# Strassen weight forms of a decoder step: summed, rounded and split in one instruction over all K tiles instead of two

## The chip, the cores and the metric

One core of a Trainium2 chip runs the whole step. The metric is the device time of one execution in microseconds (us); lower is better.

## The reference

Two layers of a decoder trunk on 512 prompt positions and 8 sample tokens, 520 columns in all, model width 2048. Cut to what matters here:

```python
h = rmsnorm(x, norm_g)
z = h @ w_in                                  # 2048 x 8192
b_c, c_c, x_c, g_c, q, k, v, g_r = split_projection(z)
conv_y, new_buf = short_conv(c_c * x_c, conv_buf, conv_w)
y_conv = b_c * conv_y * silu(g_c)
o, new_S = retention(rope(q), rope(k) * HD ** -0.5, v, ret_S, log_gamma)
y_ret = group_norm(o) * silu(g_r)
x = x + concat([y_conv, y_ret]) @ w_out       # 2048 x 2048
x = x + sigmoid(x @ w_pg) * (p_i @ w_ple)     # 2048 x 2048
```

All is float32, and after the layers comes a last RMSNorm. The outputs are the activations and the new convolution and retention states.

## The kernel before

**Products.** Activations are kept transposed: tiles of 128 of the 2048 features (K tiles, 16 of them) by 520 columns, handled as two halves of 260 columns. A float32 product is made of three TensorE matmuls on rounded operands: each operand is split into a high part (the value rounded to fp32r) and a low part (the rest), and `mm3` (L247 to L249) adds high x high, weights' high x activations' low, and weights' low x activations' high. The weights are the stationary side, 128 x 128, and each matmul streams 260 columns.

**Weights.** Weights come from HBM in rows of K tiles into `raw_ring`, a ring of 32 tiles of 128 x 128. `split_w` turns a stretch of it into the two parts: ScalarE writes the rounded high part (L229), VectorE subtracts it from the raw values and writes the low part (L230). Both parts lie in `split_ring`, a ring of 60 tiles, in contiguous stretches; a place is free again when TensorE has read it.

**Pairs.** Two blocks of 128 output features at a time are a pair. `plain` multiplies them directly, loading and splitting four K tiles at a time. `strassen` treats the first `s` K tiles as a 2 x 2 block product with the two output blocks and the two column halves, and needs seven products of `q = s / 2` K tiles instead of eight; the K tiles from `s` to 16 are done as in `plain`. Which pair uses which `s` is written out in tables at the top (`HEADS`, `CONVS`, `OUT_ROWS`, `GATES`): mostly 14 (q = 7) in the heads' pairs and 16 (q = 8) in the others, 8 or 12 in a few, and 0 (plain) where a stage begins or ends.

The seven weight operands of a pair (here called forms) are `w11`, `w12`, `w22` as loaded and four more that `add` (L319, on VectorE) makes in place in the raw ring as sums or differences. `times` then splits a form and multiplies it: q tiles x 3 matmuls, so 24 matmuls for eight tiles. Three constants set how many K tiles one instruction takes: `CHL` for a DMA load, `CHA` for `add`, `CHS` for `split_w` in `times`. All three are 4, so forms of five to eight tiles are handled in two pieces (3 + 4 for seven, 4 + 4 for eight):

```python
def chunks(a, b, most=CH):
    n = (b - a + most - 1) // most
    e = [a + (b - a) * i // n for i in range(n + 1)] if n else [a]
    return list(zip(e, e[1:]))

def times(out, raw, xs, start, more):
    for i, j in chunks(0, q, CHS):
        w = split_w(raw[:, P * i : P * j])
        product(out, w, 0, xs[i:j], start and i == 0, j == q, more)
        split_ring.put(*w)
```

**Stages and order.** Each layer runs the heads' pairs (with the retention steps placed beside them), the pairs of the convolution branch, the output projection, and the gate. The operands of the next stage (their loads, the sums of activation tiles L413 to L416 and their splits L551 and L552) are made while the last pairs of the stage ahead still run. The order of instructions on every engine is set at build time by a list scheduler that works from priorities and its own estimate of durations; splits and sums of weights are raised by `WPRIO`. On the chip each engine then works strictly in that order. The last part of the program (from L1281 on) is ordered by hand on TensorE and VectorE.

Of the kernel before, what the change touches and what calls it, by code (L numbers as in the profile page):

```python
# [28 lines left out]
EPS = 1e-6  # L29
NSLOT = 75  # L30
CH = 4
CHS = 4
CHA = 4
CHL = 4
CK = 256
BUSY = 10**9
# [155 lines left out]
def trunk_kernel(  # L192
# [32 lines left out]
    def split_w(raw, slot=False):  # L225
        n = raw.shape[1]
        hi, lo = (getr()[:, :n] if slot and not split_ring.fits(n // P) else split_ring.get(n // P) for _ in range(2))
        with tc.high_priority(offset=WPRIO):
            S.activation(hi, raw, AF.Copy)  # L229
            V.tensor_tensor(lo, raw, F(hi), SUB)  # L230
        return hi, lo
# [6 lines that stand above are left out]
# [52 lines left out]
    def strassen(x, src0, src1, s, step=None):  # L290
# [24 lines left out]
        def add(out, x, y, op):  # L315
            for i, j in chunks(0, q, CHA):
                n = slice(P * i, P * j)
                with tc.high_priority(offset=WPRIO):
                    V.tensor_tensor(out[:, n], x[:, n], y[:, n], op)  # L319
# [6 lines that stand above are left out]
# [1153 lines left out]
```

## Time and profile before

| what | value |
|---|---|
| three timed runs | 2166.78, 2166.96, 2170.64 us (median 2166.96) |
| profiled execution | span 2167.3 us, from the first to the last instruction; no other time of it is given |
| ScalarE rounds the high parts, L229 | 1347 instructions, 777.3 us |
| VectorE makes the low parts, L230 | 1346 instructions, 849.2 us |
| VectorE sums forms, L319 | 660 instructions, 428.9 us |

"Busy" is the time in which an engine had an instruction in work. Matmuls overlap each other, so a matmul's own duration (some 283 ns) is more than the distance of two of them. In the rows of groups, the number after the bar is the idle time of the engine just before these instructions, with what ended it. Line numbers are those of the kernel; PE is TensorE, PEld its weight load, DVE VectorE, ACT ScalarE, SP the queue that issues the weight loads.

### The profile page before, as it was taken

What the parts mean: (1) busy time and instruction counts of PE and PEld (TensorE: products, weight loads), DVE (VectorE), ACT (ScalarE), POOL (GpSimd) and SP (SyncE); (2) the same over time, 40 slices, a digit from 0 to 9 for tenths busy, and PEclk for the clock granted to TensorE, in tenths of its full rate; (3) what the DMA queues carried; (4) which work ended last, traced back from release to release, by engine and by line L of the source; (5) the groups of instructions that cost most, each with busy time, mean ns of one, the idle gap of its engine ahead of it and who ended that gap; (6) DMA issues with size and microseconds to landing.
All of it is one profiled execution on the core that took longest, in us unless ns stands there. A gap on an engine that the chain in (4) does not pass through costs nothing. (4 is left out here: it accounts for less than half of the span.)

```text
span 2167.3 us, 48178 instructions
## 1 busy us (share of the span) xinstructions
PE 2147.8 (99%) x17861; PEld 2142.1 (99%) x17861; DVE 1896.1 (87%) x3849; ACT 1264.5 (58%) x2647; POOL 430.6 (20%) x746
## 2 busy tenths in 40 slices
PE   9999999999999999999999999999999999999998
PEld 9999999999999999999999999999999999999998
DVE  8889988998999987987997988989999998879884
ACT  8656655565555655655765655565645555456565
POOL 2313222211001211200212222231111022011011
PEclk9999999999999999999999999999999999999999
DMA  8555565545543745645645566664464355566455
GB/s 288 171 175 197 181 217 184 178 157 175 158 129 118 238 156 187 215 154 160 215 144 175 172 213 191 189 209 170 151 182 149 120 158 202 176 207 200 128 164 198
DMA packets 182861, 387.31 MB, mean 179 GB/s; under 512 B 25888, under 2 KB 56352, under 8 KB 182624
## 3 DMA queue, kind: packets, MB, share of 16 engines
q1 hardware_dynamic: 128704, 212.98, 31.6%
q0 software_dynamic: 53056, 169.84, 23.8%
q8 instruction: 140, 2.29, 0.4%
q10 hardware_dynamic: 864, 1.39, 0.2%
q14 instruction: 97, 0.79, 0.1%
HBM read 318.96 MB, written 65.15 MB: 177 GB/s over the span
## 5 line engine op out<-in xcount | busy, mean ns | idle before, releaser
L247 PE MATMUL ps_g<-slot,split 128*128 128x260 f32 x5465 | 1531.6, 284 | 7.2 <-ACT slot L307 2.9
L248 PE MATMUL ps_g<-slot,split 128*128 128x260 f32 x5465 | 1534.3, 282 | 0.3 <-DVE slot L555 0.3
L249 PE MATMUL ps_g<-slot,split 128*128 128x260 f32 x5461 | 1519.9, 283 | 0.5 <-DVE split L230 0.5
L229 ACT ACTIVATE split<-raw 128x512 fp32r<-128x512 f32 (+2 forms) x1347 | 777.3, 596 | 583.1 <-DVE raw L319 213.2
L247 PEld LDWEIGHTS ps_g<-slot,split 128*128 128x128 f32 x5465 | 1024.0, 188 | 10.1 <-ACT slot L307 3.7
L248 PEld LDWEIGHTS ps_g<-slot,split 128*128 128x128 f32 x5465 | 1028.5, 188 | 0.5 <-DVE slot L555 0.5
L249 PEld LDWEIGHTS ps_g<-slot,split 128*128 128x128 f32 x5461 | 1019.8, 188 | 1.0 <-DVE split L230 1.0
L230 DVE TENSOR_TENSOR split<-raw,split 128x512 fp32r<-128x512 f32 (+2 forms) x1346 | 849.2, 652 | 172.5 <-PE ps_g L248 85.4
L319 DVE TENSOR_TENSOR raw<-raw 128x512 f32<-128x512 f32 (+1 forms) x660 | 428.9, 660 | 32.5 <-DMA raw<-wi 23.7
L307 ACT ACTIVATE slot<-ps_g 128x260 f32<-128x260 f32 x336 | 127.4, 381 | 140.6 <-PE ps_g L249 122.7
L551 ACT ACTIVATE slot<-slot 128x520 fp32r<-128x520 f32 (+1 forms) x212 | 109.2, 562 | 46.6 <-DVE slot L414 11.1
L552 DVE TENSOR_TENSOR slot<-slot,slot 128x520 fp32r<-128x520 f32 (+1 forms) x212 | 124.4, 620 | 4.1 <-ACT slot L551 3.9
L781 POOL DMA_DIRECT2D o_rets<-slot x64 | 35.3, 552 | 351.6 <-DVE slot L780 131.7
L307 DVE TENSOR_TENSOR slot<-ps_g,slot 128x260 f32<-128x260 f32 x168 | 70.9, 424 | 6.0 <-PE ps_g L249 3.7
L869 POOL DMA_DIRECT2D slot<-hs x64 | 46.2, 724 | 118.7 <-DVE split L230 42.7
L814 POOL DMA_DIRECT2D hs<-slot x64 | 35.6, 556 | 139.3 <-DVE slot L755 61.3
L780 DVE SCALAR_TENSOR_TENSOR slot<-slot,vs,slot 128x256 f32<-128x256 f32 x128 | 56.1, 481 | 4.5 <-ACT slot L776 4.3
L746 DVE TENSOR_TENSOR slot<-slot,slot 128x520 f32<-128x520 f32 x80 | 55.8, 698 | 4.7 <-DMA o_rets<-slot 3.7
L770 POOL DMA_DIRECT2D slot<-sret x64 | 35.5, 554 | 114.6 <-ACT split L229 37.3
L1058 POOL DMA_DIRECT2D slot<-x1s x76 | 40.8, 538 | 87.6 <-PE ps_g L249 27.2
L1209 POOL DMA_DIRECT2D x2s<-slot x30 | 16.4, 545 | 201.6 <-DVE slot L1204 200.6
L771 POOL DMA_DIRECT2D slot<-kq x64 | 34.9, 547 | 106.0 <-DVE slot L876 22.2
(217 smaller groups left out, 1733.8 us busy)
## 6 DMA issues: line engine op xcount, KB each, us to landing
raw<-wi SPq DMA_DIRECT2D x377, 256.0 KB, 3.9
raw<-wo SPq DMA_DIRECT2D x128, 256.0 KB, 5.4
raw<-wg SPq DMA_DIRECT2D x122, 256.0 KB, 4.1
raw<-wi SPq DMA_DIRECT2D x136, 192.0 KB, 4.0
slot<-x1s POOLq DMA_DIRECT2D x76, 260.0 KB, 5.1
slot<-sret POOLq DMA_DIRECT2D x64, 256.0 KB, 4.0
hs<-slot POOLq DMA_DIRECT2D x64, 256.0 KB, 4.0
slot<-hs POOLq DMA_DIRECT2D x64, 256.0 KB, 5.2
```

The source lines that it names most:

```text
L229: S.activation(hi, raw, AF.Copy)
L230: V.tensor_tensor(lo, raw, F(hi), SUB)
L247: PE.matmul(out, wh, xh, start=start, stop=False, skip_group_check=more)
L248: PE.matmul(out, wh, xl, start=False, stop=False, skip_group_check=more)
L249: PE.matmul(out, wl, xh, start=False, stop=stop, skip_group_check=more)
L307: fn(*args)
L319: V.tensor_tensor(out[:, n], x[:, n], y[:, n], op)
L551: keep(S.activation(hi, src[:, n], AF.Copy))
L552: V.tensor_tensor(lo, src[:, n], F(hi), SUB)
L746: V.tensor_tensor(out[:, n], v, table[:, n], MUL)
L780: keep(V.scalar_tensor_tensor(st[:, c], k, vs[:, h, e, b : b + 1], st[:, c], MUL, ADD))
L869: SIDE.dma_start(t[:, :512].rearrange("p (m n) -> p m n", m=2), src)
```

## The change

Two constants become 8, so that `add` and the split in `times` take a whole form of up to eight K tiles at once. `CHL` stays 4: a form is still loaded by two DMAs. Nothing else in the code changes; `plain`, the K tiles from `s` on, and pairs with four tiles a form work in pieces as before.

```diff
-CHS = 4
-CHA = 4
+CHS = 8
+CHA = 8
 CHL = 4
```

Since the scheduler orders the program anew, the order shifts in many places. Two of them follow, both on VectorE.

The first is in the convolution stage of the second layer, in a pair of eight tiles a form (around 1610 to 1618 us in the profile of before). `L319` sums forms, `L230` makes low parts, `L746` and `L1092` to `L1095` are work on the convolution's values. Before:

```order
2562 L319 TENSOR_TENSOR raw<-raw 128x512
2563 L230 TENSOR_TENSOR split<-raw,split 128x512 x2
2564 L746 TENSOR_TENSOR slot_1127_21089<-slot_1124_20859,slot_1127_21089 128x520
2565 L230 TENSOR_TENSOR split<-raw,split 128x512 x2
2566 L319 TENSOR_TENSOR raw<-raw 128x512
2567 L230 TENSOR_TENSOR split<-raw,split 128x512
2568 L1092 SCALAR_TENSOR_TENSOR slot_1128_21094<-slot_1127_21089,vec,slot_1128_21094 128x511
2569 L1094 SCALAR_TENSOR_TENSOR slot_1128_21094<-scv,vec,slot_1128_21094 128x8
2570 L319 TENSOR_TENSOR raw<-raw 128x512
2571 L230 TENSOR_TENSOR split<-raw,split 128x512
2572 L1093 SCALAR_TENSOR_TENSOR slot_1128_21094<-slot_1127_21089,vec,slot_1128_21094 128x510
```

The same place after the change:

```order
2000 L230 TENSOR_TENSOR split<-raw,split 128x1024
2001 L746 TENSOR_TENSOR slot_1127_19991<-slot_1124_19779,slot_1127_19991 128x520
2002 L319 TENSOR_TENSOR raw<-raw 128x1024
2003 L230 TENSOR_TENSOR split<-raw,split 128x1024 x2
2004 L1092 SCALAR_TENSOR_TENSOR slot_1128_19996<-slot_1127_19991,vec,slot_1128_19996 128x511
2005 L1094 SCALAR_TENSOR_TENSOR slot_1128_19996<-scv,vec,slot_1128_19996 128x8
2006 L230 TENSOR_TENSOR split<-raw,split 128x1024
2007 L1093 SCALAR_TENSOR_TENSOR slot_1128_19996<-slot_1127_19991,vec,slot_1128_19996 128x510
```

Where a sum of four tiles stood between the splits of halves, and other work between the halves of one form, now a whole form is summed and then split in one piece.

The second place is at the end of the convolution stage of the first layer (around 711 to 716 us in the profile of before), where the operands of the output projection are made: `L413` to `L416` are sums of activation tiles, `L552` their low parts. Before:

```order
1166 L230 TENSOR_TENSOR split<-raw,split 128x512
1167 L415 TENSOR_TENSOR slot_480_9348<-slot_478_9345,slot_477_9343 128x260
1168 L230 TENSOR_TENSOR split<-raw,split 128x384
1169 L552 TENSOR_TENSOR slot_469_9325<-slot_465_9253,slot_469_9325 128x260
1170 L230 TENSOR_TENSOR split<-raw,split 128x512
1171 L414 TENSOR_TENSOR slot_467_9319<-slot_466_9255,slot_467_9319 128x260
1172 L552 TENSOR_TENSOR slot_470_9326<-slot_465_9253,slot_470_9326 128x260
1173 L414 TENSOR_TENSOR slot_479_9347<-slot_478_9345,slot_479_9347 128x260
1174 L552 TENSOR_TENSOR slot_472_9332<-slot_466_9255,slot_471_9331 128x520
1175 L230 TENSOR_TENSOR split<-raw,split 128x256
```

After:

```order
900 L230 TENSOR_TENSOR split<-raw,split 128x896
901 L415 TENSOR_TENSOR slot_480_8853<-slot_478_8850,slot_477_8848 128x260
902 L552 TENSOR_TENSOR slot_469_8830<-slot_465_8765,slot_469_8830 128x260
903 L319 TENSOR_TENSOR raw<-raw 128x896
904 L414 TENSOR_TENSOR slot_467_8824<-slot_466_8767,slot_467_8824 128x260
905 L552 TENSOR_TENSOR slot_470_8831<-slot_465_8765,slot_470_8831 128x260
906 L552 TENSOR_TENSOR slot_472_8837<-slot_466_8767,slot_471_8836 128x520
907 L1093 SCALAR_TENSOR_TENSOR slot_462_8702<-slot_461_8697,vec,slot_462_8702 128x510
908 L1095 SCALAR_TENSOR_TENSOR slot_462_8702<-scv,vec,slot_462_8702 128x8
909 L414 TENSOR_TENSOR slot_479_8852<-slot_478_8850,slot_479_8852 128x260
910 L416 TENSOR_TENSOR slot_468_8825<-slot_466_8767,slot_467_8824 128x260
911 L230 TENSOR_TENSOR split<-raw,split 128x896 x2
```

Before, a split of weights came after every one or two pieces of other work; now seven pieces of operand and convolution work stand between the sum at 903 and the next two splits, which are whole forms of seven tiles.

The weight loads on SP keep their number and sizes, and TensorE keeps its number of matmuls, in another order.

## The prediction

> **What bounds the kernel now.** I read the page first, then the busy time by windows, the waits, the groups with shapes kept apart, and last the timeline at the few places where TensorE stands still.
>
> ```profile
> span 2167.3 us, 48178 instructions
> PE 2147.8 (99%) x17861; PEld 2142.1 (99%) x17861; DVE 1896.1 (87%) x3849; ACT 1264.5 (58%) x2647; POOL 430.6 (20%) x746
> ...
> 0.00:40.00 40.00, 37.24 (x281) 36.32 (x282) 30.33 (x56) 31.99 (x62) 13.34 (x32) 1.00 0.93 325
> 40.00:2100.00 2060.00, 2052.39 (x17104) 2048.58 (x17103) 1826.27 (x3707) 1193.50 (x2491) 405.35 (x693) 1.00 0.56 176
> 2100.00:2168.00 68.00, 58.17 (x481) 57.22 (x479) 39.53 (x90) 39.04 (x97) 11.95 (x21) 0.97 0.52 179
> ```
>
> TensorE is the bound. In the window from 40 to 2100 us it is busy for 2052.39 of 2060 us, at 2052.39 / 17104 = 0.120 us a matmul, at the full clock. The change leaves its number of matmuls alone. So the most that faster producers can win there is the idle rest, 2060.00 - 2052.39 = **7.6 us**, or 0.35% of the span; the start and the end hold no merged pieces worth a term. What the change can lose has no such lid: the question is whether TensorE will wait for pieces that are twice as large.
>
> Who is ahead of whom is in the waits:
>
> ```profile
> ACT split L229 <- DVE raw L319: 213.2, 160, 4.3
> ...
> ACT split L229 <- PE ps_g L249: 186.2, 220, 3.9
> ...
> DVE split L230 <- PE ps_g L248: 85.4, 109, 2.2
> ACT split L229 <- DMA raw<-wi: 75.6, 59, 3.5
> ```
>
> (Engine and line, who ended the wait, us in total, times, longest.) Both producers wait for TensorE to free places in the split ring, 220 and 109 times: they run ahead until the ring is full. The ring is the cover under which late loads and late sums cost nothing, and it stays at 60 tiles.
>
> **The change part by part. First, what it removes.** Its cost rows:
>
> ```profile
> L230 DVE TENSOR_TENSOR split<-raw,split 128x512 fp32r<-128x512 f32 x1031 | 695.0, 690 | 147.8 <-PE ps_g L248 81.2 <-ACT split L229 51.8 <-issue 6.1
> L229 ACT ACTIVATE split<-raw 128x512 fp32r<-128x512 f32 x1032 | 632.3, 626 | 462.3 <-DVE raw L319 188.2 <-PE ps_g L249 166.4 <-PE ps_g L248 45.1
> L319 DVE TENSOR_TENSOR raw<-raw 128x512 f32<-128x512 f32 x520 | 354.1, 688 | 17.6 <-DMA raw<-wi 12.1 <-DMA raw<-wo 2.9
> L230 DVE TENSOR_TENSOR split<-raw,split 128x384 fp32r<-128x384 f32 x249 | 137.1, 555 | 16.2 <-ACT split L229 9.9 <-PE ps_g L248 3.4 <-ACT slot L551 1.9
> ...
> L229 ACT ACTIVATE split<-raw 128x384 fp32r<-128x384 f32 x249 | 127.2, 518 | 84.0 <-DVE raw L319 25.0 <-PE ps_g L248 24.2 <-PE ps_g L249 17.9
> ...
> L319 DVE TENSOR_TENSOR raw<-raw 128x384 f32<-128x384 f32 x140 | 77.4, 554 | 14.9 <-DMA raw<-wi 11.6 <-DMA raw<-wg 2.8
> ...
> 499.70 1.89 DVE L230 TENSOR_TENSOR split<-raw,split 128x512 fp32r<-128x512 f32 x3
> ...
> 701.15 1.57 ACT L229 ACTIVATE split<-raw 128x512 fp32r<-128x512 f32 x3 [1.40 <-DVE raw L319]
> ```
>
> There are 520 + 140 = 660 sums of forms, four a pair and two each for pairs of more than four tiles a form: the rows give 47 pairs of eight tiles (512 twice), 33 of seven (384 and 512), one of six and three of four, which stay as they are. So 81 pairs lose 4 sums and 7 splits each: 891 instructions of VectorE and 567 of ScalarE.
>
> The time for one more tile is 690 - 555 = 135 ns on VectorE and 626 - 518 = 108 ns on ScalarE. No row shows eight tiles, so estimates: 690 + 4 x 135 = 1230 ns and 626 + 4 x 108 = 1058 ns. Against two single ones that saves 150 and 194 ns. Back to back, though, three splits of VectorE take 1.89 us and three of ScalarE 1.57, so each further one takes 0.60 and 0.47, and a merger saves only 0.06 and 0.04. VectorE is thus freed of 53 to 134 us and ScalarE of 23 to 110 us, between these two ends. Nearly all of it is worth nothing, because it lies beside matmuls.
>
> The Trainium skill has a rule for each side. "Advanced Engine Details and Errata", section The Read-Write Bubble, says that memory latency shows between instructions of these two engines, and advises operands of 512 or 1024 elements; by it alone the sum below would be zero or negative. "Perfetto Trace Analysis", section Optimizing Scalar/DVE Operations, says of engines that are not saturated but cause bubbles on others: "breaking up instructions may allow work to be completed sooner"; by it the change goes the wrong way. The trace bears the first out in the 0.06 us; the second bears on the places below.
>
> **What it adds: the ring holds fewer whole pieces.** An eight-tile piece takes 16 of the 60 tiles, half a piece 8. Before, 7 halves fit; with one being read and one being written, 5 are spare, each 12 matmuls: 60 x 0.120 = 7.2 us of cover. After, 3 whole pieces fit and one is spare: 24 x 0.120 = 2.9 us. Seven-tile pieces: 8 halves before, so 6 spare x 10.5 matmuls = 7.6 us; 4 whole ones after, 2 spare x 21 = 5.0 us. These are estimates from the 0.120 us; places freed tile by tile soften them a little. The cover falls by **4.3 us** in the eight-tile pairs and **2.6 us** in the seven-tile ones. In most of the run this costs nothing: the mean wait of a split for its sum is 213.2 / 160 = 1.3 us, under either cover. It costs where the cover runs out already.
>
> **Term 1: the change of operands from the convolutions to the output projection**, once a layer.
>
> ```profile
> 700.00:710.00 10.00, 8.80 (x73) 8.60 (x73) 10.00 (x20) 8.85 (x22) 3.74 (x7) 1.00 0.52 147
> 710.00:720.00 10.00, 10.00 (x86) 10.00 (x85) 10.00 (x25) 6.16 (x20) 3.54 (x7) 1.00 0.89 293
> 720.00:730.00 10.00, 7.88 (x64) 7.47 (x63) 10.00 (x22) 9.87 (x28) 3.29 (x7) 1.00 1.01 376
> ...
> 706.46 0.39 PE L247 MATMUL ps_g<-slot,split 128*128 128x260 f32 x1 [1.20 <-ACT ps_g L307]
> ...
> 726.13 0.39 PE L247 MATMUL ps_g<-slot,split 128*128 128x260 f32 x1 [0.83 <-ACT slot L307]
> 729.26 0.39 PE L247 MATMUL ps_g<-slot,split 128*128 128x260 f32 x1 [1.29 <-ACT split L229]
> ...
> 1787.85 0.39 PE L247 MATMUL ps_g<-slot,split 128*128 128x260 f32 x1 [1.29 <-ACT slot L307]
> 1795.74 0.39 PE L247 MATMUL ps_g<-slot,split 128*128 128x260 f32 x1 [0.56 <-ACT slot L307]
> ```
>
> (Windows: PE, PEld, VectorE, ScalarE and GpSimd busy, clock, DMA share, GB/s. Timeline: in brackets the idle time and who ended it.) From 700 to 730 us VectorE is full for 30 us, and the DMA engines are full in the last ten, since the next stage's operands are loaded, summed and split here. TensorE lives on the cover and runs out of it: 1.20 + 0.83 + 1.29 us here, 1.29 + 0.56 us in the second layer, 5.2 of the 7.6 us. The last pair ahead has seven tiles, so the stage begins with 2.6 us less cover. Against that stands that pair's own relief on VectorE: 11 mergers at 0.06 to 0.15 us, 0.7 to 1.7 us, of which I count half an us, since much of it falls ahead of the full stretch. Term: 2 x (2.6 - 0.5) = **+4.2 us**; its ends are 2 x -1.7 = -3.4 (the cover was not what mattered) and 2 x 2.6 = +5.2.
>
> **Term 2: a form whose second half lands late.** The longest pieces of the chain hold these loads:
>
> ```profile
> 1458.90 8.50 DMA raw<-wi
> ...
> 1614.61 3.28 DMA raw<-wi
> 1617.97 0.64 ACT split L229
> ...
> 1695.01 3.75 DMA raw<-wi
> ...
> 1717.32 3.63 DMA raw<-wi
> ...
> 1614.14 1.16 ACT L229 ACTIVATE split<-raw 128x512 fp32r<-128x512 f32 x2 [0.45 <-PE ps_g L249]
> 1617.97 0.63 ACT L229 ACTIVATE split<-raw 128x512 fp32r<-128x512 f32 x1 [2.67 <-DMA raw<-wi]
> ...
> 1618.65 0.39 PE L247 MATMUL ps_g<-slot,split 128*128 128x260 f32 x1 [0.24 <-ACT split L229]
> ```
>
> At 1614 us ScalarE splits what has landed, waits 2.67 us for the rest of a form, and TensorE multiplies the first half meanwhile: it idles for 0.24 us only. With one instruction the form waits for its last byte. TensorE then lacks the 12 matmuls of the first half as cover, 1.44 us, and the split lasts 1058 - 626 = 0.43 us longer: 1.9 us for each such load that finds the cover spent. Of the four loads in the chain I charge two (TensorE idled after the one at 1614, and the one at 1717 lies in the same run of loads): **+3.8 us**. Ends: 0, if none is late again, and 4 x 1.9 = +7.6.
>
> The loads themselves are unchanged in number and size, but a raw region is now free for its next load only when the whole piece has been read. That is up to one half-split later, about 0.6 us, hidden as long as the cover is not spent; I price it inside term 2.
>
> **Sum:** 2167.3 + 4.2 + 3.8 = 2175.3 us against the profiled execution. Its span is 0.3 us over the median of the three timed runs, 2166.96, and the profile gives no other time of it; so the forecast for the median is **2175 us**, 0.4% slower. The ends of the terms give -3.4 to +12.8.
>
> **The rivals.**
>
> *The relief wins (faster).* ScalarE ends most of the large waits quoted above with a copy out of PSUM (L307), which stands in its queue behind splits and operand work; if fewer instructions bring these copies and VectorE's operand work forward in the two full stretches, the idle time there shrinks. This decides if a stretch contains more saving than cover lost: it needs over 2.6 us, so more than 17 mergers at the best price of 0.15 us, and the pair ahead has 11. Its most is all 7.6 us, 2159; a likely case is two thirds of it, 2162. The Trainium skill's section The Read-Write Bubble speaks for it. Chance 0.10.
>
> *Nothing to be measured.* The scheduler sets the order anew, the late loads move, and the remaining cover of 2.9 to 5.0 us is enough but for an us or two: 2167 to 2170 us. For it speaks the mean wait of 1.3 us; against it that 5.2 us are lost with a cover of over 7 us already. Chance 0.28. This kernel's runs tell about 0.2%, 4.3 us, from no change.
>
> *The steady stretch fails (much slower).* If the single spare piece of the eight-tile pairs (2.9 us) is spent in each of them, because a sum waits for its load and the split for its sum (longest waits 4.3 and 3.5 us), each of the 47 pairs stalls. At 0.4 us apiece, 47 x 0.4 = 19 us: 2186. Against it: the means are far under 2.9 us, and VectorE has more free time than before. Chance 0.14.
>
> **How the numbers follow.** The forecast's own case, stalls at the changes of operands and at late loads, from 2171.4 to 2181, has 0.48. Slower by over 0.2% is this case and the steady stretch, 0.62; within 0.2% is 0.28; faster is 0.10. The range reaches from just under no change to the steady stretch at its price, 2164 to 2187, and leaves out most of the faster case and the far end of the slowest.
>
> **What would show it.** Right: TensorE's busy time stays at about 2148 us, its idle time between 40 and 2100 us grows from 7.6 to about 15 us, the growth lies around 700 to 730 and 1780 to 1800 us and behind a few raw loads, and ends in ScalarE's splits or copies; VectorE's busy time falls by 53 to 134 us without any use. Step one is wrong if an eight-tile split lasts other than about 1.23 and 1.06 us. Term 1 is wrong if the two stretches stall no more than now; term 2 if late loads are followed by no idle TensorE; all of it if short stalls come back in every eight-tile pair.

## The result and the profile after

The changed kernel takes 2229.85 us (median of four runs, 2223.70 to 2233.24) beside 2168.47 us for the kernel before: a ratio of 1.0273, 95% interval 1.0249 to 1.0298. It is **slower by 61 us**. The sign was forecast and the size was not: 2175 us, with a range that ended at 2187. The profiled execution is the shortest of the four runs, 2223.7 us with a span of 2221.7; what the views below say is about this run, whose span is 54 us longer than that of before.

The page and the busy time by windows (us of the stretch, then PE, PEld, VectorE, ScalarE and GpSimd busy with their instructions, clock, DMA share, GB/s):

```profile
span 2221.7 us, 45853 instructions
...
PE 2173.9 (98%) x17861; PEld 2152.6 (97%) x17861; DVE 1835.9 (83%) x2958; ACT 1184.0 (53%) x2080; POOL 434.9 (20%) x746
...
0.00:40.00 40.00, 38.28 (x282) 37.77 (x283) 30.50 (x56) 32.05 (x62) 13.36 (x32) 1.00 0.92 328
40.00:2150.00 2110.00, 2074.99 (x17091) 2055.95 (x17090) 1766.03 (x2823) 1111.95 (x1926) 409.50 (x693) 1.00 0.54 171
```

What the change removes came as worked out: VectorE has 3849 - 2958 = 891 instructions fewer, ScalarE 2647 - 2080 = 567. VectorE's busy time fell by 60.2 us, ScalarE's by 80.5. But TensorE's idle time in the long middle rose from 7.6 to 2110.00 - 2074.99 = **35.0 us**, and its busy time for about the same 17,100 matmuls rose too, from 2052.39 to 2074.99 us. The latter isn't work: the first matmul behind a stop counts 0.39 us and more (rows below), where a fed one starts 0.12 us after its neighbour; and a few microseconds are the clock (last section). A stop therefore costs more than the idle time that the profile puts ahead of it.

The waits, in the columns of before:

```profile
ACT split L229 <- DVE raw L319: 288.4, 123, 6.8
...
DVE split L230 <- ACT split L229: 156.4, 177, 5.0
...
DVE split L230 <- PE ps_g L248: 97.0, 58, 3.7
ACT split L229 <- DMA raw<-wi: 95.2, 64, 4.3
ACT split L229 <- PE ps_g L248: 86.4, 69, 5.4
...
ACT split L229 <- PE ps_g L249: 35.7, 22, 4.5
...
PE ps_g L247 <- ACT split L229: 16.4, 21, 2.4
```

ScalarE's waits for a free place in the split ring fell from 186.2 + 74.4 = 260.6 to 35.7 + 86.4 = 122.1 us. Its waits for sums rose from 213.2 to 288.4 us, in fewer and longer pieces, and VectorE's for ScalarE from 69.3 to 156.4. VectorE's waits for a place fell in number, from 109 to 58, but not in total (85.4 to 97.0 us). Before, the producers mostly ran ahead until the ring was full; now they wait for each other more, and run into a full ring less often. TensorE's wait for ScalarE's splits ends up in the list, 21 times.

Where the time is lost shows in the number of matmuls that TensorE gets through in equal stretches of the clock. Two of them, of before and then of after:

```profile
1150.00:1500.00 350.00, 349.33 (x2921) 348.83 (x2920) 311.56 (x692) 207.39 (x458) 89.03 (x151) 1.00 0.59 187
...
500.00:700.00 200.00, 200.00 (x1672) 200.00 (x1671) 181.12 (x359) 106.14 (x213) 23.30 (x32) 1.00 0.48 144
```

```profile
1150.00:1500.00 350.00, 336.96 (x2748) 333.27 (x2747) 282.25 (x485) 180.32 (x328) 89.73 (x152) 0.99 0.56 177
...
500.00:700.00 200.00, 197.43 (x1613) 194.09 (x1612) 174.26 (x256) 96.67 (x146) 24.43 (x34) 1.00 0.44 137
```

At 0.120 us a matmul, the heads of the second layer (1150 to 1500) lose 173 x 0.120 = **20.8 us**, the convolutions of the first (500 to 700) 59 x 0.120 = 7.1 us. (The changed kernel falls further behind as it runs, so equal stretches don't hold quite the same work.) The same count over all of the middle is in the table of the second group of experiments.

**Two kinds of stop.** The first is in the heads of the second layer. Timeline of the changed kernel at two of its largest stops:

```profile
1196.67 1.09 DVE L230 TENSOR_TENSOR split<-raw,split 128x896 fp32r<-128x896 f32 x1
...
1197.78 0.81 SPq L312 DMA_DIRECT2D raw<-wi  x2
...
1204.18 0.95 ACT L229 ACTIVATE split<-raw 128x896 fp32r<-128x896 f32 x1 [1.64 <-DMA raw<-wi]
...
1205.18 0.58 PE L247 MATMUL ps_g<-slot,split 128*128 128x260 f32 x1 [2.08 <-ACT split L229]
...
1418.41 1.09 DVE L230 TENSOR_TENSOR split<-raw,split 128x896 fp32r<-128x896 f32 x1
...
1419.52 0.82 SPq L312 DMA_DIRECT2D raw<-wi  x2
...
1424.87 2.63 ACT L229 ACTIVATE split<-raw 128x896 fp32r<-128x896 f32 x3 [3.17 <-DMA raw<-wi]
...
1425.87 0.39 PE L247 MATMUL ps_g<-slot,split 128*128 128x260 f32 x1 [2.44 <-ACT split L229]
```

And the DMA issues of the two moments (count, KB, us from issue to landing):

```profile
raw<-wi SPq DMA_DIRECT2D x1, 256.0 KB, 5.9
...
raw<-wi SPq DMA_DIRECT2D x1, 256.0 KB, 4.9
```

Both times the two loads of a form are issued 0.02 us after the low part of a whole form has ended (1196.67 + 1.09 = 1197.76, 1418.41 + 1.09 = 1419.50). The second of them goes out some 0.4 us later and lands after 5.9 and 4.9 us, at 1204.1 and 1424.8. There ScalarE goes on, and TensorE, which has long run dry, 1.0 us later. A region of the raw ring comes free only when the whole piece has been read; the load starts late, and nothing covers it. At the first of the two stops the cover was already spent: ScalarE's two splits ahead of the late one began at 1200.74, after 2.32 us of waiting for TensorE to free a place in the split ring.

The second kind is in every pair of the convolutions between 500 and 700 us. Timeline of one (`L1093` and `L1095` are work on the convolution's values):

```profile
596.61 1.22 DVE L230 TENSOR_TENSOR split<-raw,split 128x1024 fp32r<-128x1024 f32 x1
597.74 0.75 DVE L1093 SCALAR_TENSOR_TENSOR slot<-slot,vec,slot 128x510 f32<-128x510 f32 x1
598.40 0.22 DVE L1095 SCALAR_TENSOR_TENSOR slot<-scv,vec,slot 128x8 f32<-128x8 f32 x1
598.54 1.22 DVE L319 TENSOR_TENSOR raw<-raw 128x1024 f32<-128x1024 f32 x1
...
599.79 1.06 ACT L229 ACTIVATE split<-raw 128x1024 fp32r<-128x1024 f32 x1 [1.80 <-DVE raw L319]
...
597.88 0.39 PE L249 MATMUL ps_g<-slot,split 128*128 128x260 f32 x1
...
600.91 0.39 PE L247 MATMUL ps_g<-slot,split 128*128 128x260 f32 x1
```

The sums are made in place: `w21` is overwritten by w21 + w22, then by w22 - w11, then by w12 - w21. So a sum can't begin before the low part of the form in the same region has been made. This is tight once a pair: the third form follows the second at once, while two other products stand between the third and `w12 - w21`. Here the low part ends at 597.83, and TensorE starts on it 0.05 us later; the next sum begins at 598.54 and ends at 599.76, its rounding ends at 600.85, and TensorE starts on that 0.06 us later. Low part, sum, rounding: 1.22 + 1.22 + 1.06 = 3.50 us of instructions for one form, one behind the other on two engines, against 24 x 0.120 = 2.88 us of matmuls. With halves the same work can overlap, one half with ScalarE while the other is with VectorE. This was a reading of the trace; the experiments tried it.

### The profile page after: what moved, and what is told of

Read it like the earlier page. It is cut to its first block, busy times and chain, and to the rows that moved or that the text cites. A ratio compares the mean times of both kernels' runs of the same rounds, so it can differ in the third digit from the quotient of the medians.

```text
span 2221.7 us, 45853 instructions
## 1 busy us (share of the span) xinstructions
PE 2173.9 (98%) x17861; PEld 2152.6 (97%) x17861; DVE 1835.9 (83%) x2958; ACT 1184.0 (53%) x2080; POOL 434.9 (20%) x746
## 5 line engine op out<-in xcount | busy, mean ns | idle before, releaser
L230 DVE TENSOR_TENSOR split<-raw,split 128x1024 fp32r<-128x1024 f32 (+4 forms) x780 | 777.9, 1013 | 272.0 <-ACT split L229 156.4
L229 ACT ACTIVATE split<-raw 128x1024 fp32r<-128x1024 f32 (+4 forms) x780 | 679.3, 886 | 572.1 <-DVE raw L319 288.4
L319 DVE TENSOR_TENSOR raw<-raw 128x1024 f32<-128x1024 f32 (+2 forms) x336 | 385.4, 1147 | 27.7 <-DMA raw<-wi 15.1
L552 DVE TENSOR_TENSOR slot<-slot,slot 128x520 fp32r<-128x520 f32 (+1 forms) x212 | 124.4, 622 | 9.2 <-ACT slot L551 9.0
L746 DVE TENSOR_TENSOR slot<-slot,slot 128x520 f32<-128x520 f32 x80 | 55.8, 698 | 1.8 <-DMA o_retp<-slot 1.1
L307 ACT ACTIVATE ps_g<-ps_g 128x260 f32<-128x260 f32 x121 | 45.1, 373 | 21.8 <-PE ps_g L249 20.0
```

Of the source, the lines that this page charges most:

```text
L307: fn(*args)
L552: V.tensor_tensor(lo, src[:, n], F(hi), SUB)
L746: V.tensor_tensor(out[:, n], v, table[:, n], MUL)
```

## The experiments

All kernels compute the same values; times are medians of four runs (other counts are named), and ratios are against the kernel before, run beside them at 2167 to 2169 us.

### One part of the change at a time, and more room

**split_only**: only the splits are whole.

```diff
-CHA = 8
+CHA = 4
```

> Splits take a whole form, sums stay in two pieces. Raw-ring theory (a raw region is free for its next load only when the whole form has been read, and load, sum and split then follow each other in whole forms: the round trip through four regions becomes the bound): most of the loss stays, 2200 to 2220 us. Split-ring theory (fewer whole pieces fit into 60 tiles): all of it stays, 2220 to 2235. Order theory (the new order happens to be a bad one): any time, with stalls at other places.

**sum_only**: only the sums are whole.

```diff
-CHS = 8
+CHS = 4
```

> Sums take a whole form, splits stay in two pieces. Raw-ring theory: only one link of the round trip is longer, and regions are read in halves as before: 2168 to 2185 us. Split-ring theory: as before, 2165 to 2172. Order theory: any time.

**ring64**: the change with a larger split ring.

```diff
-SPLIT = 60
+SPLIT = 64
```

> The change with a split ring of 64 tiles instead of 60, so that four whole eight-tile pieces fit instead of three. Split-ring theory: most of the loss is gone, 2170 to 2190 us, and TensorE's idle time between 40 and 2150 us falls from 35 to under 15. Raw-ring theory: no more than 10 us better than the change, 2213 to 2232.

**raw40**: the change with one more region of eight tiles in the raw ring, for which the split ring has to give up four.

```diff
-RAW = 32
+RAW = 40
-SPLIT = 60
+SPLIT = 56
```

> The change with a raw ring of 40 tiles (five regions of eight instead of four); the split ring gives up four tiles for it (56), which leaves three whole eight-tile and four whole seven-tile pieces in it as in the change. Raw-ring theory: most of the loss is gone, 2170 to 2190 us, ScalarE's waits for sums fall from 288 to under 150 us and its waits for TensorE to free the split ring grow again. Split-ring theory: 2220 to 2240.

| | median us | ratio (95%) |
|---|---|---|
| split_only | 2250.15 | 1.0375 (1.0357 to 1.0392) |
| sum_only | 2191.15 | 1.0106 (1.0091 to 1.0121) |
| ring64 | 2208.25 | 1.0188 (1.0169 to 1.0206) |
| raw40 | 2231.59 | 1.0293 (1.0277 to 1.0308) |

The parts don't add up: whole splits alone cost 82 us, more than the change; whole sums alone cost 23. Both lie above every range that was named for them. Four more tiles in the split ring give back 22 of the 61 us, so the ring's room counts, but isn't all of it: 2208 us lies between the ranges of the two theories. raw40 as a whole speaks against a short raw ring as the one cause. Its waits say why the total hides something:

```profile
ACT split L229 <- DVE raw L319: 281.8, 103, 8.0
...
ACT split L229 <- DMA raw<-wi: 35.5, 17, 4.2
```

The late loads of the first kind are nearly gone (95.2 to 35.5 us), and the waits for sums are not.

### The chain of sums

To test the second kind, the third sum gets a region of its own, so that it waits for no low part, and `w21` is given back early.

```diff
+        u = raw_ring.get(q)
+        add(u, w22, w11, SUB)
...
+        raw_ring.put(w21)
...
-        add(w21, w22, w11, SUB)
-        times(a, w21, t2, False, True)
+        times(a, u, t2, False, True)
...
-        add(w21, w12, w21, SUB)
+        add(u, w12, u, SUB)
...
-        times(b, w21, at(ops, k2, RIGHT), False, True)
-        raw_ring.put(w21)
+        times(b, u, at(ops, k2, RIGHT), False, True)
+        raw_ring.put(u)
```

**apart32** is the changed kernel with this edit.

> The change, with the third sum of a pair (w22 - w11) written to a free region of the raw ring instead of over the second one (w21); its region then takes w12's load. Chain theory (sums are made in place, so the sum for the third form waits until the second form has been split by both engines, and with whole forms ScalarE and VectorE take turns instead of overlapping): at least 12 us better than the change, 2190 to 2215 us, and ScalarE's waits for sums fall from 288 us to under 230. Ring theory (only the number of whole pieces in the split ring counts): 2222 to 2235.

**apart40** also has the rings of raw40 (40 raw, 56 split).

> The same with a raw ring of 40 and a split ring of 56 tiles, so that w12 need not wait for a region. Chain theory: better than the run with 40 raw tiles alone (2231.6) by at least 12 us, 2190 to 2217 us. Ring theory: 2225 to 2240.

**before_apart32** is the kernel before with the edit.

> The kernel before, with the third sum in a region of its own. Halves overlap on the two engines already, so by the chain theory little is won: 2162 to 2170 us. By the ring theory nothing: 2165 to 2171.

**before_raw40** is the kernel before with 40 raw and 56 split tiles.

> Control: the kernel before with 40 raw and 56 split tiles, in halves. Seven halves of eight tiles and seven-tile pairs' halves fit as before. Chain theory and ring theory both: 2163 to 2173 us; if it is over 2180, the 56 tiles cost something by themselves and the runs with 40 raw tiles have to be read against it.

**before_apart40** has both (seven runs).

> The kernel before with 40 raw and 56 split tiles and the third sum in a region of its own, in halves. Chain theory: the halves overlapped already, so 2160 to 2170 us, at best a few us under before (its TensorE idles 7.6 us between 40 and 2100 us, which is the most that can be won). Ring theory: 2163 to 2173.

| rings, order of sums | with pieces of four: us, ratio (95%) | with whole forms: us, ratio (95%) | cost of whole forms |
|---|---|---|---|
| 32 / 60, in place | 2168.47 | 2229.85, 1.0273 (1.0249 to 1.0298) | +61 |
| 40 / 56, in place | 2184.29, 1.0073 (1.0058 to 1.0088) | 2231.59, 1.0293 (1.0277 to 1.0308) | +47 |
| 40 / 56, third sum apart | 2171.23, 1.0018 (1.0007 to 1.0029) | 2185.05, 1.0082 (1.0061 to 1.0102) | **+14** |
| 32 / 60, third sum apart | 2187.83, 1.0091 (1.0075 to 1.0106) | 2272.45, 1.0479 (1.0449 to 1.0509) | +85 |

apart32 went the opposite way from what was expected: a pair now holds a region more, the raw ring has none to spare, and ScalarE's wait for loads became the larger one, 214.8 us (151.4 with pieces of four, 75.6 in the kernel before):

```profile
ACT split L229 <- DMA raw<-wi: 214.8, 116, 6.1
ACT split L229 <- DVE raw L319: 144.9, 73, 6.5
```

With the region there (apart40) both waits are small, 27.3 and 114.8 us, and ScalarE waits for room in the split ring again, as producers do that are ahead:

```profile
ACT split L229 <- PE ps_g L248: 199.6, 143, 4.4
...
ACT split L229 <- DVE raw L319: 114.8, 71, 7.1
...
ACT split L229 <- DMA raw<-wi: 27.3, 17, 4.5
```

So the edit that breaks one link of the chain is worth 46.5 us to the whole forms (raw40 to apart40) and 13 us to pieces of four (before_raw40 to before_apart40). That is 33 us more, far outside the intervals. Two controls missed their ranges as well: before_raw40, at 2184 us, is over the 2180 us beyond which the 56 tiles were to count as a cost of their own, and before_apart32 is 17 us over its range, with longer waits for loads. The matmuls lost by whole forms in each stretch, against the control with the same rings and order (from windows like those quoted above):

| stretch, us | 32 / 60, in place | 40 / 56, in place | 40 / 56, third sum apart |
|---|---|---|---|
| 140 to 325, heads, layer 1 | 58 | 121 | 78 |
| 325 to 1150 | 107 | 129 | 24 |
| 1150 to 1500, heads, layer 2 | 173 | 33 | 0 |
| 1500 to 2100 | 82 | 104 | -22 |
| sum, at 0.120 us | 420, 50 us | 387, 46 us | 80, 10 us |

The room in the raw ring removes the first kind of stop where it was worst: in the heads of the second layer the loss falls from 173 to 33 matmuls. The edit of the sums removes nearly all that is left there and in the stretches of the convolutions, the output projection and the gate. The heads of the first layer are not healed by either; the loss there rises with the rings of 40 and 56. Differences of a few tens of matmuls say little: the -22 is the control's doing, whose profiled run, the longest of its seven, has a granted clock of 0.57 from 1816 to 1824 us.

### How much the cover is worth

**before_ring40**, **before_ring48** and **before_ring64** (eleven runs): the kernel before with a split ring of 40, 48 and 64 tiles.

> The kernel before with a split ring of 40 tiles instead of 60: five half pieces fit, three are spare (36 matmuls, 4.3 us), less than the two whole spare pieces of a seven-tile pair in the change (5.0 us). Ring theory: at least 15 us slower than before, 2183 to 2220 us. Chain theory: the halves still overlap and little is lost, 2167 to 2180 us.

> The kernel before with a split ring of 48 tiles: six halves fit, four are spare, 48 matmuls or 5.8 us (before 7.2, with 40 tiles 4.3 and 61 us slower). Ring theory (lateness of the splits is spread over several us, so each us of cover taken away lays more of it bare): between the two, 2180 to 2210 us. If the cover only matters under some threshold near 4.3 us: under 2175.

> The kernel before with a split ring of 64 tiles: eight halves fit, six are spare, 72 matmuls or 8.6 us instead of 7.2. Ring theory (48 tiles cost 51 us, 40 cost 61): at most its 7.6 us of idle time are left to win, 2160 to 2168 us. It is also the control for the change with 64 tiles (2208.25): if halves with 64 tiles take 2165 us, the change costs 43 us there instead of 61.

| split ring | 40 | 48 | 60 | 64 |
|---|---|---|---|---|
| median us | 2229.79 | 2219.67 | 2168 | 2167.56 |
| ratio (95%) | 1.0281 (1.0264 to 1.0298) | 1.0241 (1.0223 to 1.0258) | 1 | 0.9991 (0.9982 to 1.0000) |

This is far dearer than was expected, and it is the plainest fault of the forecast. By its own count (halves of 8 tiles that fit, less two, at 1.44 us) a ring of 48 has 4 spare halves, 5.8 us, and 40 has 3, 4.3 us. Even halves lose 51 us with 5.8 us of cover, while I let whole forms live on 2.9 to 5.0 us for almost nothing. Nor is the count of whole pieces the right measure: 56 tiles hold as many halves of eight-tile forms as 60 do, and yet 40 raw and 56 split tiles cost 16 us. The larger ring gains nothing that can be measured on the kernel before, and is the only version here that isn't slower. With 64 tiles whole forms cost 2208.25 - 2167.56 = 41 us, instead of 61.

### Order, and which engine's instruction matters

**after_pre8**: the change with another early order (`PRE`, which sets how early a stage's operands are made), to see how much of the loss is the order alone.

```diff
-PRE = 9
+PRE = 8
```

> Control on the order: the change with one planner constant altered (operands of the next stage are begun with 8 instead of 9 free slots kept), which reorders some 5 per cent of VectorE's instructions and no more work. Order theory (the new order is a chance result): the time scatters by 20 us or more around the change's 2229.85. Chain and ring theory: within 10 us of it, 2220 to 2240.

It takes 2234.05 us, 1.0308 (1.0293 to 1.0324): a second order loses as much as the first, and 4 us is what this change of order makes.

**act_whole**, **dve_whole** and **region_only**: sums in halves; the ring's places are handed out for a whole form, and inside it ScalarE alone, VectorE alone, or neither takes the form in one instruction. The edit of act_whole; dve_whole has the 8 and the 4 exchanged, region_only has 4 twice:

```diff
-CHA = 8
+CHA = 4
...
-            S.activation(hi, raw, AF.Copy)
-            V.tensor_tensor(lo, raw, F(hi), SUB)
+            for i, j in chunks(0, n // P, 8):
+                k = slice(P * i, P * j)
+                S.activation(hi[:, k], raw[:, k], AF.Copy)
+            for i, j in chunks(0, n // P, 4):
+                k = slice(P * i, P * j)
+                V.tensor_tensor(lo[:, k], raw[:, k], F(hi[:, k]), SUB)
```

> Forms are summed in halves; ScalarE rounds a whole form in one instruction, VectorE makes the low part in two. Chain theory (the loss comes from the two engines taking turns on whole forms): one of the two links is short again, so clearly less than with both whole (2250.15), 2185 to 2225 us. If the size of ScalarE's piece alone carries the loss (TensorE's first matmul of a form waits for the whole rounded part): 2235 to 2255.

> Forms are summed in halves; ScalarE rounds in two instructions, VectorE makes the low part of a whole form in one. Chain theory: as above, 2185 to 2225 us. If VectorE's piece alone carries the loss (the raw region and the next in-place sum wait for the whole low part): 2235 to 2255. If ScalarE's piece alone carries it: under 2180.

> Sums in halves; places in the split ring are handed out for a whole form (eight contiguous tiles for the high and eight for the low part) and taken back as a whole, but each engine still writes them with two instructions. Chain theory (sum, rounding and low part of a form, then the next sum in place: about 2.4 us a form in halves against 2.88 us of matmuls, and 2.9 to 3.5 us as soon as one of the three takes the form whole): 2165 to 2182 us. If the handing out of places is what costs (a whole form needs eight neighbouring places that TensorE has read through): 2230 to 2255, as with whole splits.

| | median us | ratio (95%) |
|---|---|---|
| region_only | 2190.11 | 1.0101 (1.0084 to 1.0118) |
| act_whole | 2240.14 | 1.0329 (1.0315 to 1.0344) |
| dve_whole | 2257.44 | 1.0408 (1.0385 to 1.0431) |
| split_only (both) | 2250.15 | 1.0375 (1.0357 to 1.0392) |

Handing out ring places by the whole form costs 23 us by itself (with the order that comes with it), with no instruction merged. A whole instruction on either one of the two engines brings the loss to 72 and 89 us, and a second one adds nothing. This fits a chain in which either engine can be the long link; it doesn't fit a loss that is VectorE's or ScalarE's alone. All three lie above what the chain theory expected of them. act_whole lies in the range that was named for ScalarE's piece as the one cause, but under that cause dve_whole should have stayed under 2180 us. And by the chain alone split_only, with its shorter sums, should lose less than the change; it loses 21 us more. So the chain's length alone doesn't give the sizes.

## Why the prediction was wrong

**The mergers' worth: right.** The durations of eight tiles were estimated at 1230 and 1058 ns; groups of the changed kernel with shapes kept apart:

```profile
L230 DVE TENSOR_TENSOR split<-raw,split 128x1024 fp32r<-128x1024 f32 x329 | 399.4, 1223 | 141.7 <-ACT split L229 75.9 <-PE ps_g L248 57.9 <-ACT slot L1091 3.8
L229 ACT ACTIVATE split<-raw 128x1024 fp32r<-128x1024 f32 x329 | 346.0, 1057 | 277.5 <-DVE raw L319 184.6 <-PE ps_g L248 34.1 <-DMA raw<-wi 26.4
...
L319 DVE TENSOR_TENSOR raw<-raw 128x1024 f32<-128x1024 f32 x188 | 229.6, 1221 | 9.7 <-DMA raw<-wg 6.7 <-DMA raw<-wi 1.4 <-DMA raw<-wo 0.7
```

They took 1223 and 1057 ns. The freed time is inside its ends on both engines, and it bought nothing, as forecast. Of the two rules quoted from the Trainium skill, that of "Perfetto Trace Analysis", section Optimizing Scalar/DVE Operations, was the one for this kernel: VectorE and ScalarE were not saturated (87 and 58% busy), and larger instructions on them made bubbles on TensorE: its idle time in the long middle rose from 7.6 to 35.0 us, and the kernel lost 61.

**The cover: the step that failed.** "In most of the run this costs nothing: the mean wait of a split for its sum is 213.2 / 160 = 1.3 us, under either cover." The fall of the cover from 7.2 to 2.9 us was worked out and then charged at two places only. A mean wait that is measured with the cover in place doesn't say what happens without it: the waits were short because the producers were ahead. What should have been set against the cover is the chain that makes one form out of the one before it, 3.50 us in whole pieces against 2.88 us of matmuls, plus the work of other kinds that VectorE has queued between its links (0.71 us in the pair above). Its parts all stood in the prediction, as durations and as the in-place sums of the code; they were not put one behind another. The runs show the cover's price (before_ring48, +51 us) and, as far as that edit stands for the chain alone, the chain's share (the cost of whole forms falls from 47 to 14 us once a link is broken and the raw region is there).

**A raw region that comes free later: right in kind, wrong in size.** It was called "hidden as long as the cover is not spent" and priced inside term 2 at +3.8 us for two late loads. The late loads with TensorE idle behind them are there, in the heads of the second layer instead of behind 1614 and 1717 us, and that stretch lost 20.8 us in all, of which raw40 leaves 33 x 0.120 = 4.0 against its own control.

**Term 1, the change of operands: right in kind, too large.** The stretches in which VectorE is full lie later in the changed kernel, at 717 to 745 and 1820 to 1850 us. Their busy time by windows, and the stops in them:

```profile
717.00:745.00 28.00, 23.58 (x189) 22.67 (x188) 28.00 (x56) 22.23 (x58) 9.12 (x18) 1.00 0.76 257
1820.00:1850.00 30.00, 26.84 (x218) 26.00 (x217) 30.00 (x62) 22.55 (x60) 8.02 (x15) 1.00 0.76 264
...
720.68 0.39 PE L247 MATMUL ps_g<-slot,split 128*128 128x260 f32 x1 [0.89 <-ACT ps_g L307]
...
726.59 0.39 PE L247 MATMUL ps_g<-slot,split 128*128 128x260 f32 x1 [0.60 <-ACT slot L307]
...
731.09 0.39 PE L247 MATMUL ps_g<-slot,split 128*128 128x260 f32 x1 [1.22 <-ACT split L229]
...
742.31 0.39 PE L247 MATMUL ps_g<-slot,split 128*128 128x260 f32 x1 [1.71 <-ACT slot L307]
...
1822.57 0.39 PE L247 MATMUL ps_g<-slot,split 128*128 128x260 f32 x1 [0.85 <-ACT ps_g L307]
1829.08 0.39 PE L247 MATMUL ps_g<-slot,split 128*128 128x260 f32 x1 [1.24 <-ACT split L229]
1830.20 0.39 PE L247 MATMUL ps_g<-slot,split 128*128 128x260 f32 x1 [0.61 <-ACT slot L307]
...
1846.15 0.39 PE L247 MATMUL ps_g<-slot,split 128*128 128x260 f32 x1 [0.46 <-ACT slot L307]
```

These are 4.42 and 3.16 us, 7.6 in both layers, against 5.2 before: 2.4 us more, where the term had 4.2. Whether the smaller cover or the new order makes them is not shown. They are a small part of the 35.0 - 7.6 = 27.4 us by which the idle time rose, so where TensorE idled already was no guide to where most of the loss would fall.

**The rival of the steady stretch** came nearest: "short stalls come back in every eight-tile pair" was named as what would overturn the forecast, and in the convolutions they do. Over 500 to 700 us a pair takes about 20.8 us, so the 7.1 us are 0.7 us a pair, where the rival had 0.4. It was given 0.14, on the strength of the same mean wait, and it left out the seven-tile pairs, where more was lost.

**What stays open.** Why whole splits with halved sums (split_only, +82) and VectorE's split alone (dve_whole, +89) lose more than the change (+61); the order may be a part, and a part is the clock: the mean granted clock of the profiled runs is 0.993 in both, against 0.997 in the change, which is 0.007 x 2250.9 - 0.003 x 2221.7 = 9 us of the 29 by which split_only's profiled run is longer. Neither was tried by itself. Why a split ring of 60 loses nothing to 64 and 48 loses 51 us. What holds the heads of the first layer back in apart40, 78 matmuls or 9 us; a granted clock of 0.98 over these 185 us accounts for some 0.02 x 185 / 0.120 = 31 of them. And apart40 differs from raw40 in the order, and in the earlier return of `w21`, as well as in the link, so that the 33 us belong to the edit as a whole; that the two engines' instructions wait along that chain is read from the trace.

## What to carry to other kernels

Before merging instructions on engines that feed a saturated one, add up the chain that makes one item, over all engines and queues it crosses, and set that against the time the consumer takes for the item; a merged piece lengthens the chain by what no longer overlaps and shrinks the cover by what no longer fits. A short mean wait and a low busy share of the producers don't tell this, since both are measured with the cover in place: run the kernel once with a smaller ring to learn what the cover is worth. Buffers that are updated in place and regions given back by the piece are links of this chain, as much as the engines are.

## What the hardware showed that was not expected

TensorE's clock fell although TensorE was never idle for long. Windows of the changed kernel around the stop at 1205 us and the stops up to 1428:

```profile
1201.60:1205.10 3.50, 1.04 (x7) 0.63 (x5) 2.09 (x2) 1.86 (x4) 0.00 (x0) 1.00 0.82 270
1205.10:1208.50 3.40, 3.32 (x15) 3.32 (x16) 0.76 (x2) 0.91 (x4) 0.00 (x0) 0.51 0.87 277
...
1424.20:1427.70 3.50, 1.07 (x4) 0.59 (x4) 1.00 (x1) 2.83 (x5) 0.54 (x1) 0.90 0.53 203
1427.70:1434.50 6.80, 6.67 (x33) 6.67 (x34) 3.53 (x7) 1.69 (x5) 0.00 (x0) 0.55 0.76 241
```

In each of two stretches of 3.5 us TensorE was busy for about 1.05 us, and in the next 3.4 and 6.8 us the granted clock was 0.51 and 0.55: 15 matmuls where 3.40 / 0.120 = 28 would go, and 33 where 57 would. The two cost (13 + 24) x 0.120 = 4.4 us on top of the stops. In the long middle of the kernel before, the clock stays full. The Trainium skill, "TensorE: Matmul & The Clock Gate", section What's actually happening, has the clock at half after an idle window of some 3.4 us; the half agrees, and the slow stretches are about one and two such windows long, but here a stretch of that length with a few matmuls in it was enough.
